# The convolution layer taken in two halves, its MLP under another kind of norm, and a new order of issue at the end of the Fourier layer

## The chip, the cores and the metric

One Trainium2 chip, all 8 cores (two dies of four). Each core computes two of the sixteen sequences and never talks to another core. The metric is the device time of the slowest core, in microseconds (us). A program on all cores falls now and then into a slower state, in which the cores of one die are granted a lower TensorE clock; each run is therefore sorted into fast or slow, and only fast runs are compared. Engines are called as in the profile: PE (matmuls), PEld (its weight loads), DVE (vector engine), ACT (scalar engine), POOL (GpSimd), SP (the engine that issues most transfers here).

## The reference

Four residual layers with the mixers pool, conv, Fourier, pool; behind each mixer there is an MLP with a squared ReLU; each of the two parts has an RMS norm in front. `x` is (16, 2048, 1024). The parts that matter here:

```python
def rms_norm(x, g):
    y = x * lax.rsqrt(jnp.mean(x * x, axis=-1, keepdims=True) + NORM_EPS)
    return y * g

def conv_module(h, w_in, dw, dw_bias, ln_g, ln_b, w_out):
    val, gate = jnp.split(h @ w_in, 2, axis=-1)          # 1024 -> 2 x 1024
    v = val * jax.nn.sigmoid(gate)                       # GLU
    v = depthwise_conv(v, dw) + dw_bias                  # 31 taps, centred, over positions
    mu = jnp.mean(v, axis=-1, keepdims=True)             # LayerNorm over ALL channels
    var = jnp.mean(jnp.square(v - mu), axis=-1, keepdims=True)
    vn = (v - mu) * lax.rsqrt(var + LN_EPS) * ln_g + ln_b
    return jax.nn.silu(vn) @ w_out

def fourier_mixer(h, w_in, w_out):
    u = (h @ w_in).reshape(b, s, 4, 256)
    return jnp.fft.fft2(u, axes=(1, 3), norm='ortho').real.reshape(b, s, d) @ w_out

def sq_relu_mlp(h, w_up, w_down):
    a = jax.nn.relu(h @ w_up)                            # 1024 -> 4096
    return (a * a) @ w_down
# ... (pool mixer, parameters and the loop over the layers cut)
```

The kernel uses bf16 operands with f32 accumulation.

## The kernel before

A sequence lies in SBUF as X, 8 channel chunks of 128 partitions by 2048 positions in f32; work goes by position tiles of 512 (`j` = 0 to 3). A helper records every operation, works out the semaphores, and emits them in the order of the Python calls, one queue for each engine. So the order of calls below is the order on each engine.

The MLP goes through the hidden width in four slabs; a step is one slab of one tile. `up` makes relu squared, `down` adds into X. The norm comes in two kinds. Kind "norm": the tile's statistics must be known first, then eight DVE instructions write scaled copies of X (x times gain times 1/rms) that the matmuls read. Kind "mlp": the matmuls read copies that carry only the gain (`x_chunk`, made as soon as X is written), and since relu squared of a scaled input is relu squared times the square of the scale, the norm is put on afterwards, as a factor `r2` on every down product.

```python
class Mlp:
    def up(self, i, count=FCS):
        # ... (fetch the slab's weights; kind "norm" waits for the statistics here)
        for fc in range(lo, hi):
            bank = b.bank()
            for kc in range(DC):
                b.mm(bank, wu[kc // 4][...], b.Hk(n, j, kc), kc == 0, kc == DC - 1)
            t = b.T.next()
            b.act(t, bank, AF.Relu)
            b.tt(a[:, fc, :], t, t, ALU.mult)
    def down(self, i):
        # ...
        for dc in range(DC):
            # ... (eight matmuls into bank)
            t = bank
            if n.kind == "mlp":
                t = b.TM.next()
                b.tt(t, bank, r2, ALU.mult)
            b.tt(b.X[:, dc, sl], b.X[:, dc, sl], t, ALU.add)
    def run(self):
        b.pump(2); self.up(0)
        for i, (k, j) in enumerate(self.steps):
            if n.kind == "mlp" and k == 0 and j not in n.ready:
                b.x_ready(n, j)               # squares of X on ACT, sums on DVE
            if i + 1 < len(self.steps):
                self.up(i + 1)
            self.down(i)
            # ... (prefetch of weights)
```

The conv layer runs chunk by chunk over all four tiles. The convolution needs each value on shifted partitions, so a chunk's GLU output goes to scratch in DRAM (`scr_v`) and comes back. LayerNorm needs every channel of a tile, hence the tail: sums, normalize (subtract, multiply, Silu) and the output projection come when all convolutions are done.

```python
def conv_layer(self, s, li):
    # ... (glu: 16 matmuls, sigmoid on ACT, product on DVE; spread: write to and read back from scratch)
    for c in range(1, DC - 2):
        # ... build_diag(c - 1); glu(c, j) for all four tiles
        for h in range(2):
            for j in range(h * HT, (h + 1) * HT):
                conv(c - 1, j, v4[h])
            spread(c, h, v4[h])
    # ... (the last two chunks)
    ln_sums(0); ln_rstd(0)
    conv(ca, 2, v4[1]); ln_sums(1); normalize(0, 1)
    # ...
    out(0, lambda: [f() for f in late])       # projection, six banks open at a time
    out(1)
    self.x_ready(self.nxt, 0)
    out(2)
    out(3)
    for j in range(1, NT):
        self.x_ready(self.nxt, j)
```

The end of the Fourier layer interleaves its last projections with the first up products of its MLP:

```python
    for oc in range(DC):
        out_step(1, oc)                       # 9 matmuls, then four adds on DVE
        for j in (1, 2, 3):
            self.x_chunk(nx, j, oc, eng="act")
        self.M.up(0, 1)                       # 8 matmuls, relu on ACT, square on DVE
```

Of the kernel before, what the change touches and what calls it, by code (L numbers as in the profile page):

```python
# [103 lines left out]
def const_tables():  # L104
# [4 lines left out]
    M[:, lay["mask"]:lay["mask"] + 32] = np.tile(np.eye(32), (4, 1))  # L109
# [208 lines left out]
class Mlp:  # L318
    def __init__(self, bld, s, li, n, nxt, order, ahead):
        self.b, self.s, self.li, self.n, self.nxt, self.order, self.ahead = bld, s, li, n, nxt, order, ahead  # L320
        self.steps = [(k, j) for k in range(NSLAB) for j in order]
        self.ups, self.downs, self.fc = {}, {}, {}
        self.A = None

    def up(self, i, count=FCS):
# [13 lines left out]
        for fc in range(lo, hi):  # L339
# [5 lines left out]
            b.tt(a[:, fc, :], t, t, ALU.mult)  # L345
        if hi == FCS and lo < FCS:
            if j == self.order[-1]:
                b.release(self.ups[k])
# [3 lines left out]
    def down(self, i):  # L352
# [23 lines left out]
        if j == self.order[-1]:  # L376
            b.release(self.downs[k])

    def run(self):
# [3 lines left out]
        for i, (k, j) in enumerate(self.steps):  # L383
            if n.kind == "mlp" and k == 0 and j not in n.ready:
                b.x_ready(n, j)
            if i + 1 < len(self.steps):
                self.up(i + 1)
# [10 lines left out]
class Builder:  # L398
# [88 lines left out]
    def make_plan(self):  # L487
# [8 lines left out]
        for s in range(self.nseq):  # L496
            for li, kind in enumerate(KINDS):
# [20 lines left out]
                elif kind == "conv":  # L518
                    win, wo = W[f"l{li}_conv_w_in"], W[f"l{li}_conv_w_out"]
                    for c in range(0, DC, 2):  # L520
                        add(("cin", s, li, c), 1, [
                            ("pool", 0, v * DC * 512, BF16, (DC, 256),
                             rows(win[:, v * D + c * 128:v * D + (c + 2) * 128]), None) for v in range(2)])
                    add(("cwo", s, li), 2, [("pool", h, 0, BF16, (4, D), rows(wo[h * 512:(h + 1) * 512, :]), None)
                                            for h in range(2)])
# [42 lines left out]
    def pump(self, reserve, ahead=6):  # L568
        while (self.w_i < len(self.plan) and len(self.w_got) < ahead and self.plan[self.w_i][0][0] not in ("cwo", "ftab")
               and len(self.freeb) - self.plan[self.w_i][1] >= reserve):  # L570
            self.w_issue()
# [123 lines left out]
    def out_tile(self, j, w, src, eng="dve", lazy=False, hook=None):  # L695
        sl = slice(j * TT, (j + 1) * TT)
        n = self.nxt
        for oc in range(DC):
# [7 lines left out]
        if not lazy:  # L706
# [137 lines left out]
    def conv_layer(self, s, li):  # L844
# [3 lines left out]
        L = HT * TT + 8  # L848
        miscb = self.alloc()
# [8 lines left out]
        acc1b = self.alloc()  # L858
        ACC1 = self.buf(acc1b, F32, (NT, TT))
# [4 lines left out]
        mask = self.cm("mask", 32)  # L864

        def Cv(c, j):
            return self.buf(Cb[c // 2, j // 2], F32, (2, 2, TT))[:, j % 2, c % 2, :]

        def SLv(c, j):
            return self.buf(Cb[c // 2, j // 2], BF16, (2, 2, 2 * TT))[:, j % 2, c % 2, 0:TT]  # L870

        def V4(b, q):
            return self.buf(b, BF16, (4, L))[:, q, :]

        def build_diag(c):
            dwc = self.VEC[:, dwo + c * 32: dwo + (c + 1) * 32]
            self.tt(DGs[c % 2], mask.unsqueeze(1).broadcast_to([128, 32, 32]),
                    dwc.unsqueeze(2).broadcast_to([128, 32, 32]), ALU.mult)

        def win(c):  # L880
            if c // 2 not in slab:
                slab[c // 2] = self.w_get(("cin", s, li, c // 2 * 2))[0]
            return self.buf(slab[c // 2], BF16, (2, DC, 256))[:, :, :, (c % 2) * 128:(c % 2) * 128 + 128]

        def glu(c, j):
            self.need_stat(n, j)
            w = win(c)
# [6 lines left out]
            self.act(sg, bg, AF.Sigmoid)  # L894
            self.tt(Vc[c % 2][:, CONV_PAD + j * TT:CONV_PAD + (j + 1) * TT], bv, sg, ALU.mult)

        def vwrite(c, h):
            w = slice(h * (HT + 1) * TT, VW if h else (HT + 1) * TT)
            self.dma("sp", f"vs{h}", (s, c), self.scr["v"][c % 2][:, w], Vc[c % 2][:, w], writes=[f"v{c % 2}{h}"])

        def vread(c, h, b):
            sc = self.scr["v"][c % 2]
            v4 = self.buf(b, BF16, (4, L))
            for sh in (0, 2, 1, 3):
                src = bass.AP(sc.tensor, sc.offset + h * HT * TT + 8 * sh, [[VW, 32], [32 * VW, 4], [1, L]])
                self.dma("sp", f"v{c % 2}{h}", (s, c), v4[32 * sh:32 * sh + 32], src,
                         reads=[f"v{c % 2}{h}", f"v{c % 2}0"])

        def spread(c, h, b):
            vwrite(c, h)  # L910
            vread(c, h, b)

        def conv(c, j, b, late=None):
            h = j // HT
            if (c // 2, h) not in Cb:
# [556 lines left out]
```

## Time and profile before

| before | value | from |
|---|---|---|
| time, median of 3 runs | 4976.78 us (4974.51 to 5418.52) | the timed runs |
| span of an undisturbed core | about 4964 us, middle one | cores without a dip of the clock, all calls |
| PE busy | 96% | busy line of the page |
| all waits of PE, core 5 | 182 us | its waits |
| clock granted, core 5 | 0.985 | the cores view |
| one full matmul (512 columns) in a dense stretch | 215.8 ns | 400 of them start within 86.3 us |

PE sets the end. "Clock" is the mean clock that TensorE was granted, as a share of full speed. In every view a line such as L407 is that of a helper: 407 is any matmul, 421 any ACT instruction, 424 a two-input DVE or POOL instruction, 428 a one-input one, 432 (438 in the kernel after) a scaled product with three inputs, 442 (448) a memset. In the kernel after, the numbers of the first four are 413, 427, 430 and 434. "arena" is SBUF, "ps" is PSUM.

### The profile page before, as it was taken

Reading aid. Unit: us, or ns where it says so; the run is one execution under the profiler, and the core shown is the slowest. Engines: PE = TensorE matmul, PEld = TensorE weight load, DVE = VectorE, ACT = ScalarE, POOL = GpSimd, SP = SyncE. Lnnn points to the kernel's source line nnn. Section 1 sums busy time; section 2 is a strip of 40 time slices with the busy share of each in tenths; the row PEclk is TensorE's granted clock in tenths of the full one; section 3 lists DMA queues with packets and bytes.
Section 4 is the critical chain, followed back from the end, with each engine's and each line's share of the span. In section 5 each row is a group of like instructions: output and inputs, shape, how many; then the busy total and the mean of one; then the engine's idle time right before and its main releaser. Section 6 shows DMA issues by size and latency. Waiting matters only on the chain.

```text
span 5030.9 us, 67432 instructions; the slowest of 8 cores (4954.5 to 5030.9 us)
## 1 busy us (share of the span) xinstructions
PE 4828.7 (96%) x24270; PEld 2190.0 (44%) x24270; DVE 2647.5 (53%) x3948; ACT 1456.5 (29%) x2139; POOL 197.0 (4%) x218
## 2 busy tenths in 40 slices
PE   7999999899998999999999999979998899999998
PEld 3444444344443444444444444434443344444443
DVE  2433454756655667443455435466657465645345
ACT  4311234611234113411253113353112321233112
POOL 0000000100010000000000000010000000000000
PEclk7888999999999999999999999989999999999999
DMA  7312125411034220512142230444201421123201
GB/s 155 62 34 34 18 56 132 76 34 34 9 112 76 43 42 9 101 34 34 40 145 51 42 43 1 120 84 76 38 22 53 67 43 34 26 34 56 46 1 67
DMA packets 147460, 274.61 MB, mean 55 GB/s; under 512 B 6848, under 2 KB 33600, under 8 KB 145088
## 3 DMA queue, kind: packets, MB, share of 16 engines
q0 software_dynamic: 98752, 164.11, 19.6%
q1 hardware_dynamic: 48384, 106.19, 7.2%
q8 instruction: 202, 3.31, 0.3%
q14 instruction: 122, 1.00, 0.1%
HBM read 398.59 MB, written 33.69 MB: 86 GB/s over the span
## 4 chain that ended last, share of the span: by engine, by line
PE 88%; DVE 5%; DMA 3%; ACT 2%; issue 2%; SPq 0%; POOL 0%; DVEq 0%; ACTq 0%; POOLq 0%
PE ps L407 88%; DVE arena L424 4%; ACT arena L421 2%; DVE arena L432 1%; DMA arena<-l_pool_w_in 1%; DMA arena<-xT 0%; DMA arena<-l_pool_w_out 0%; DMA arena<-scr_v 0%; DMA scr_v<-arena 0%; DMA arena<-l_mlp_up 0%; SPq L445 0%; POOL arena L445 0%; DVE arena L428 0%; ACT L421 0%; DVEq L285 0%
## 5 line engine op out<-in xcount | busy, mean ns | idle before, releaser
L407 PE MATMUL ps<-arena 128*128 128x512 bf16 (+5 forms) x24270 | 4828.7, 377 | 185.4 <-ACT arena L421 67.4
L407 PEld LDWEIGHTS ps<-arena 128*128 128x128 bf16 (+1 forms) x24270 | 2190.0, 99 | 2823.6 <-issue 520.5
L424 DVE TENSOR_TENSOR arena<-arena 128x512 f32<-128x512 f32 (+5 forms) x2044 | 1426.2, 707 | 1285.7 <-ACT arena L421 1208.7
L421 ACT ACTIVATE arena<-ps 128x512 f32<-128x512 f32 (+2 forms) x1368 | 788.0, 596 | 2618.3 <-PE ps L407 2505.7
L424 DVE TENSOR_TENSOR arena<-arena,ps 128x512 f32<-128x512 f32 (+2 forms) x834 | 555.5, 683 | 717.3 <-PE ps L407 697.4
L421 ACT ACTIVATE arena<-arena 128x512 bf16<-128x512 f32 (+3 forms) x490 | 493.0, 1037 | 697.3 <-DVE arena L424 676.5
L424 DVE TENSOR_TENSOR arena<-ps,arena 128x512 f32<-128x512 f32 (+1 forms) x584 | 402.4, 690 | 226.0 <-PE ps L407 202.9
L432 DVE SCALAR_TENSOR_TENSOR arena<-arena 128x512 bf16<-128x512 f32 (+1 forms) x320 | 215.5, 745 | 62.9 <-ACT arena L421 61.2
L421 ACT ACTIVATE arena<-ps,arena 128x512 bf16<-128x512 f32 (+2 forms) x264 | 167.4, 663 | 221.1 <-PE ps L407 204.2
L445 POOL DMA_DIRECT2D arena<-l_mlp_up x64 | 47.8, 750 | 1479.6 <-PE ps L407 1199.6
L445 POOL DMA_DIRECT2D arena<-l_mlp_down x64 | 48.0, 753 | 1405.3 <-PE ps L407 1020.0
L428 DVE TENSOR_SCALAR arena<-arena 128x512 bf16<-128x512 f32 (+1 forms) x144 | 62.7, 470 | 60.9 <-DMA arena<-xT 40.4
L424 POOL TENSOR_TENSOR arena<-arena 128x512 f32<-128x512 f32 (+1 forms) x36 | 61.9, 1722 | 219.1 <-ACT arena L421 158.4
L421 ACT ACT_TABLE_LOAD x17 | 21.8, 1283 | 26.9 <-DMA arena<-xT 14.2
L445 POOL DMA_DIRECT2D arena<-l_conv_w_out x4 | 3.0, 748 | 555.5 <-PE ps L407 555.5
L445 POOL DMA_DIRECT2D arena<-l_conv_w_in x16 | 14.0, 894 | 215.7 <-PE ps L407 215.7
L445 POOL DMA_DIRECT2D arena<-l_pool_w_in x14 | 11.1, 804 | 175.5 <-PE ps L407 174.4
L439 DVE COPY arena<-arena 128x512 f32<-128x512 f32 (+1 forms) x12 | 4.1, 345 | 25.1 <-ACT arena L421 25.1
L442 POOL MEMSET arena<- 128x1024 bf16 (+1 forms) x6 | 4.0, 702 | 280.5 <-DVE arena L424 280.5
L445 POOL DMA_DIRECT2D arena<-l_pool_w_out x4 | 3.0, 759 | 38.9 <-PE ps L407 38.9
L445 POOL DMA_DIRECT2D arena<-l_fourier_w_inT x2 | 1.5, 744 | 67.9 <-PE ps L407 67.9
L445 POOL DMA_DIRECT2D arena<-l_fourier_w_out_x x2 | 1.1, 542 | 72.7 <-DVE arena L424 72.7
(6 smaller groups left out, 2.8 us busy)
## 6 DMA issues: line engine op xcount, KB each, us to landing
arena<-l_mlp_up POOLq DMA_DIRECT2D x64, 1024.0 KB, 11.7
arena<-l_mlp_down POOLq DMA_DIRECT2D x64, 1024.0 KB, 11.3
arena<-scr_v SPq DMA_DIRECT2D x128, 258.0 KB, 4.9
arena<-xT SPq DMA_DIRECT2D x32, 512.0 KB, 8.6
outT<-arena SPq DMA_DIRECT2D x16, 1024.0 KB, 4.3
arena<-l_conv_w_in POOLq DMA_DIRECT2D x16, 512.0 KB, 10.9
arena<-dfts SPq DMA_DIRECT2D x8, 1024.0 KB, 6.2
scr_v<-arena SPq DMA_DIRECT2D x16, 384.0 KB, 2.5
```

Of the source, the lines that this page charges most:

```text
L407: self.P.add("pe", lambda e: e.matmul(out, lhsT, rhs, start=start, stop=stop, skip_group_check=skip), reads=[lhsT, rhs], writes=[out])
L421: self.P.add("act", lambda e: e.activation(out, in_, func, **kw), reads=reads, writes=[out])
L424: self.P.add(eng, lambda e: e.tensor_tensor(out, in0, in1, op), reads=[in0, in1], writes=[out])
L428: self.P.add(eng, lambda e: e.tensor_scalar(out, in0, s1, None, op0), reads=reads, writes=[out])
L432: self.P.add(eng, lambda e: e.scalar_tensor_tensor(out, in0, scalar, in1, op0, op1), reads=reads, writes=[out])
L439: self.P.add(eng, lambda e: e.tensor_copy(out, in_), reads=[in_], writes=[out])
L442: self.P.add(eng, lambda e: e.memset(ap, val), writes=[ap])
L445: return self.P.add(q, lambda e: e.dma_start(out=out, in_=in_), reads=[in_] + list(reads), writes=[out] + list(writes), chan=chan, group=g ...
```

## The change

Its intent has three parts.

1. **Conv layer in two halves.** Tiles 0 and 1 are convolved for all chunks first; then the GLU of tile 3 and the convolutions of tiles 2 and 3 run beside LayerNorm, normalize and projection of the first half, so that PE has matmuls while DVE and ACT work. Sigmoid becomes a tanh (sigmoid(g) = (1 + tanh(g/2))/2, with the half put into the convolution's mask). The diagonals and more of the subtracts go to POOL. The output weights come in two slabs of columns.
2. **The MLP after the conv layer takes kind "norm"**: eight scaled copies per tile before its matmuls, no product on the down banks. Its first up products move into the end of the conv layer to fill holes there. The tile order (0, 3, 1, 2) is left to the last slab.
3. **End of the Fourier layer**: weights asked for earlier, relu before the copies on ACT, the square after the next projection's adds on DVE; in `run`, half of the next up products before the squares of `x_ready`.

```diff
@@ the tables
-    M[:, lay["mask"]:lay["mask"] + 32] = np.tile(np.eye(32), (4, 1))
+    M[:, lay["mask"]:lay["mask"] + 32] = np.tile(0.5 * np.eye(32), (4, 1))
@@ Mlp.up
-            b.tt(a[:, fc, :], t, t, ALU.mult)
+            sq = lambda o=a[:, fc, :], t=t: b.tt(o, t, t, ALU.mult)
+            if later is None:
+                sq()
+            else:
+                later.append(sq)
@@ Mlp.run
-            if n.kind == "mlp" and k == 0 and j not in n.ready:
-                b.x_ready(n, j)
             if i + 1 < len(self.steps):
+                self.up(i + 1, FCS // 2)
+                if n.kind == "mlp" and k == 0 and j not in n.ready:
+                    b.x_ready(n, j)
                 self.up(i + 1)
@@ conv_layer: glu
-            self.act(sg, bg, AF.Sigmoid)
-            self.tt(Vc[c % 2][...], bv, sg, ALU.mult)
+            self.act(sg, bg, AF.Tanh, scale=0.5)
+            self.stt(Vc[c % 2][...], sg, 1.0, bv, ALU.add, ALU.mult)
@@ conv_layer: the second half (what it replaces is cut)
+        ln(0)
+        stepB(0)                      # two convolutions of the second half, diagonal, read back
+        normalize(0, 0, 2)
+        gluB(2)                       # GLU of tile 3, write to scratch
+        stepB(1)
+        normalize(0, 2, 4)
+        # ... (on in this pattern)
+        gluB(1)
+        normalize(0, 6, 8)
+        stepB(4)
+        cwo += self.w_get(("cwo", s, li, 1))
+        out(0, 0, 4, lambda oc: normalize(1, oc, oc + 1))
+        stepB(5)
+        out(0, 4, 8, lambda oc: normalize(1, oc, oc + 1))
+        # ... (prefetch)
+        stepB(6)
+        out(1, 0, 4)
+        self.need_stat(self.nxt, 0)   # statistics and the eight scaled copies of tile 0
+        stepB(7)
+        self.M.up(0, 2)               # first up products of the MLP
+        ln(1)
+        out(1, 4, 8, lambda oc: normalize(2, 2 * oc - 8, 2 * oc - 6))
+        self.M.up(0)
+        out(2, 0, 4, lambda oc: normalize(3, oc, oc + 1))
+        self.need_stat(self.nxt, 1)
+        out(2, 4, 8, lambda oc: normalize(3, oc, oc + 1))
+        self.M.up(1)
+        out(3, 0, 4)
+        self.need_stat(self.nxt, 2)
+        out(3, 4, 8)
@@ four_layer
+        self.pump(2, 1)
         for st in dft_steps(0):
...
+        later = []
         for oc in range(DC):
             out_step(1, oc)
+            if later:
+                later.pop(0)()
+            self.M.up(0, 1, later)
             for j in (1, 2, 3):
                 self.x_chunk(nx, j, oc, eng="act")
-            self.M.up(0, 1)
+        later.pop(0)()
@@ build
-                    row.append(Norm(f"l{li}_norm_mlp", "norm" if kind == "pool" else "mlp", s))
+                    row.append(Norm(f"l{li}_norm_mlp", "mlp" if kind == "four" else "norm", s))
```

Cut: the allocation of buffers, the slabs of the weights, the loops of the first half.

## The prediction

> **What bounds the kernel now.** I read the cores view first, then the page's busy lines, then, on one undisturbed core, the waits of the tensor engine, its busy time by stage, and the timelines where it sits idle.
>
> ```profile
> core 3: 5030.9 us, clock 0.967
> ...
> core 5: 4954.5 us, clock 0.985
> ...
> die 0 (median of its cores): 5022.4 us, clock 0.970
> die 1 (median of its cores): 4966.0 us, clock 0.982
> ```
>
> The profile fell in the slow state: die 0 ran at a lower clock. The fast runs (4976.78 and 4974.51 us) look like die 1, so all stage readings below are of core 5. The page (core 3) says who sets the end:
>
> ```profile
> PE 4828.7 (96%) x24270; PEld 2190.0 (44%) x24270; DVE 2647.5 (53%) x3948; ACT 1456.5 (29%) x2139; POOL 197.0 (4%) x218
> ```
>
> PE is the bound, and the change leaves every matmul in place: the same GLU, convolution, projection and MLP products, in another order. So what can be gained is only time in which PE stands still, and time in which it runs at a reduced clock. The waits of PE on core 5 (engine, line, waited for: total us, times, longest) say how much standing there is:
>
> ```profile
> PE ps L407 <- ACT arena L421: 66.8, 37, 7.0
> PE ps L407 <- DVE arena L424: 56.7, 28, 11.8
> PE ps L407 <- DMA arena<-l_pool_w_in: 16.2, 2, 15.5
> PE ps L407 <- DVE arena L442: 12.6, 2, 10.2
> PE ps L407 <- DMA arena<-scr_v: 12.6, 5, 4.2
> ...
> PE ps L407 <- DMA arena<-l_mlp_up: 5.8, 2, 3.6
> ```
>
> All rows together are 182 us. The clock adds 4954.5 x (1 - 0.985) = 74 us. Everything else, some 4700 us, is matmul streaming and fixed. By stage, core 5 (from:to, length, PE busy, PEld, DVE, ACT, POOL, then the PE clock):
>
> ```profile
> 627.00:779.00 152.00, 145.93 (x1244) 66.92 (x1248) 65.32 (x92) 53.12 (x82) 1.50 (x2) 0.99 0.59 136
> 779.00:905.00 126.00, 99.61 (x598) 41.56 (x591) 87.60 (x117) 88.98 (x117) 28.06 (x25) 0.91 0.36 66
> 1328.00:1362.00 34.00, 24.32 (x268) 16.95 (x266) 30.93 (x63) 17.44 (x34) 0.54 (x1) 0.80 0.42 137
> 1410.00:1500.00 90.00, 75.86 (x412) 34.35 (x410) 51.81 (x80) 39.59 (x62) 5.20 (x7) 0.94 0.51 82
> 3071.00:3228.00 157.00, 149.86 (x1293) 69.15 (x1296) 66.14 (x98) 54.30 (x84) 1.50 (x2) 0.98 0.58 135
> 3228.00:3355.00 127.00, 97.09 (x561) 40.34 (x554) 87.88 (x118) 89.01 (x118) 28.51 (x25) 0.91 0.35 64
> 3775.00:3815.00 40.00, 18.05 (x105) 7.98 (x103) 33.90 (x71) 10.12 (x13) 0.54 (x1) 0.74 0.31 97
> 3865.00:3945.00 80.00, 67.12 (x370) 30.38 (x369) 46.41 (x71) 36.16 (x56) 5.20 (x7) 0.94 0.57 93
> ```
>
> Each core does two sequences, so each stage stands twice. Idle is length minus busy; lost to the clock is length x (1 - clock).
> - Conv layer (rows 1, 2, 5, 6): idle 6.1 + 26.4 + 7.1 + 29.9 = 69.5, clock 1.5 + 11.3 + 3.1 + 11.4 = 27: 97 us. Nearly all is in its end (LayerNorm, normalize, output projection), where DVE and ACT are each some 70% busy and wait on each other in chains.
> - Start of the Fourier layer (rows 3, 7): idle 9.7 + 22.0, clock 6.8 + 10.4: 49 us.
> - End of the Fourier layer (rows 4, 8): idle 14.1 + 12.9, clock 5.4 + 4.8: 37 us.
>
> That is 183 of the 256 us; the rest (first loads, last norm, pool layers) the change does not touch.
>
> [...]in the rows with idle the mean clock is 0.74 to 0.94, in dense stages 1.00[...]. [...]the page of before has 17 loads of mean 1283. [...]Here a 128x512 f32 tensor_tensor takes 1373 ns on POOL and 723 on DVE.
>
> **The change, part by part.**
>
> *1. Conv layer in halves.* Now all four position tiles of all eight channel chunks are convolved before LayerNorm begins, and the projection then has no other matmul beside it. The new order does chunks 0 to 7 for the first half (tiles 0 to 2 of the GLU feed it), then interleaves the second half's GLU and convolutions with LayerNorm, normalize and projection of the first. The durations here come from the groups by shape: 20972 full matmuls in 4648.4 us at a clock of 0.967 make 0.214 us each. Per interleaved pair PE has 16 of them = 3.4, plus two convolution tiles. Those: 2048 small matmuls busy 122.4 us, so 32 take 1.9, two take 3.8. Sum 7.2 us. DVE in that time: GLU product 0.69, four running sums 4 x 0.72, one subtract and two multiplies 2.2: 5.8. ACT: tanh 0.6, four convolution reads 2.6, two Silu 1.5: 4.7. Both fit. The scratch trip (write, read back, median landings 2.5 and 4.9 us; some 12 us from the last GLU matmul to the first convolution) has 3.4 + 10.2 = 13.6 us of GLU before its first use and 10.7 or more later. So the five waits on it should go or fall under 1 us. Tanh instead of sigmoid avoids a table switch at each alternation; the half goes into the mask at no cost. POOL takes the diagonal builds and more subtracts.
>
> *2. The MLP after conv changes its norm.* Before, it scaled each down product by the norm on DVE: 8 instructions for each of 16 steps, two sequences, 256 x 0.69 = 177 us of DVE, beside matmuls that take 1.7 us each group. Now eight scaled copies per tile (8 x 0.67 = 5.4 us DVE) come before its first matmul (eight of them took 5.38 in the timeline). The MLP itself gains nothing in its middle, as PE is already full there. But at its end DVE is behind: on core 5 PE finishes at 3778.7 and DVE drains the last bank only at 3785.7. With 0.69 instead of 1.38 us per bank this 7 us backlog shrinks to 1, so the Fourier layer's inputs are ready some 6 us earlier.
>
> *3. End of the Fourier layer.* There the loop period is 5.5 us (x_chunk copies before the relu on ACT, its square before the next adds on DVE), while PE needs 17 x 0.213 = 3.6; PE runs out of banks. The new order (relu before copies, square after the next adds) leaves DVE 5 x 0.70 = 3.5 us and ACT 2.7. The earlier issue of the weights takes away the 3.6 and 2.2 us on l_mlp_up.
>
> *What remains in the conv layer, per sequence (estimates).*
> - Second half of the output weights: issued by POOL only after the diagonal that follows a convolution; about 2.5 + 9.6 to landing against 10.6 us of matmuls: 2 idle, 1 clock.
> - First MLP tile: after 10.6 us of PE work the stat matmul, then table load 1.3, Ln and Exp 1.3, DVE already 1 us late, eight copies 5.4, against 3.8 of convolution and a first group of 1.7: 3.6 idle, 1.7 clock.
> - Second LayerNorm behind the same DVE queue: 1.
> - Second MLP tile: the same chain behind Silu and a table load, against 6.8 us of matmuls: 4.7 idle, 2 clock.
> - First convolution: 1.
>
> Together 17 us, 34 for two.
>
> *Sum.* Conv 97 - 34 = 63. Fourier end 37 - 4 = 33. Fourier start: 5.5 idle and 3.5 clock of the second sequence, some 7 and 4 of the first, where the backlog also holds the banks of the setup matmuls: 20. Total 116 us, and 4977 - 116 = 4861.
>
> **The rivals.**
> - *The end of the conv layer becomes DVE-bound.* From the first projection on, DVE has 32 adds (22), 24 multiplies and 4 subtracts (20), 12 sums (9), 24 copies (16), four square reductions of 2.55 (10) and 16 relu squares (11): 88 us, against PE's 54.6 + 11.5 + 27.3 = 93. At 95% in-order coupling can cost far more than I charge. If each of three tiles waits its full chain of some 10 us, cold clock included, little of the conv gain is left: about 4920. For: the table. Against: two weight groups of the MLP are moved there to fill just this hole.
> - *Tanh is not in Silu's set.* Then five alternations bring ten loads, 13 us of ACT per layer, and ACT's 4.7 per pair grows to 7.3 against 7.2: up to 10 us per layer, 4880.
> - *The scratch trip or the weights stay exposed*, as one order on one queue now carries all of them: 3 to 4 us per hit plus clock, 4875.
> - *The filling is perfect*: nothing of the 34 left, and the Fourier start gains more: 4815.
>
> **Range and chances.** The 2% line is 4877, only 16 us from my centre, and the conv remainder of 34 is the softest term; it would have to be 50 to lose the line. The Fourier end I trust within 5 us, the start within 8. Range 4825 to 4908; faster by over 2% 0.68, within 2% 0.31, slower 0.01, as nothing new is long enough to cost more than 183 us.
>
> **What would show it.** Right: PE's waits on an undisturbed core fall from 182 to about 105 us, its clock rises from 0.985 to about 0.992, waits on l_mlp_up vanish, those on scr_v fall to a few us, DVE busy falls by some 150 us, the 128x512 bf16 scaled copies of a norm go from 256 to 320 (and 64 GLU products join that group), the Fourier start still shows some 16 us idle in the second sequence. Wrong: table loads far above 30, PE waiting 7 us or more on DVE's scaled copies before the first MLP groups, or on l_conv_w_out, or the Fourier loop still at 5 us a turn. A clock of 0.81 in both dies for long would void the comparison, not the reasoning.

What no trace or run of this case shows is cut from this text: a rule for the clock with a price per us of idle, a filing of functions in tables, and a ratio for POOL. (The 17 loads that it names are table loads of ACT.) The clock terms for what is foreseen are estimates. Where they rest on idle, they agree with the rows of before: 128 us of idle and 55 of clock are 0.43 us of clock for each us of idle, so 0.9, 1.5 and 2.0 for the idle of 2, 3.6 and 4.7 us, where it has 1, 1.7 and 2; at the Fourier start 17.2 for 31.7 are 0.54, so 6.8 for the 12.5 us of idle that it expects to go, where it has 7.5. That tanh avoids table switches was assumed; e4 counts them.

## The result, and the profile after

The kernel after takes 4893.29 us (median of 10 runs, 4890.16 in the fastest), before 4976.89 us in the same rounds. The ratio of the fast runs is 0.9833, 95% interval 0.9821 to 0.9844: 1.7% less time, inside the 2% band, to which the prediction had given 0.31 (and 0.68 to a gain of more than 2%). Ratios here are the mean time of one kernel's fast runs over that of the other's of the same rounds, so not quite the ratio of the medians. The outputs are correct.

So the predicted 4861 was 32 us too low, though inside its range (4825 to 4908), and of the 116 us that were expected 84 came. By spans of undisturbed cores (cores whose mean clock shows no dip), which leave out how the slowest of eight is drawn, it is 4964 to 4887: 77 us.

The profile after is of core 4. The busy line of the page:

```profile
PE 4753.1 (97%) x24270; PEld 2164.4 (44%) x24270; DVE 2506.7 (51%) x3724; ACT 1415.5 (29%) x2077; POOL 283.5 (6%) x262
```

The same 24270 matmuls, DVE busy 141 us less (150 foreseen). The waits of PE on core 4 (engine, line, waited for: total us, times, longest):

```profile
PE ps L413 <- ACT arena L427: 27.7, 25, 3.0
...
PE ps L413 <- DVE arena L430: 17.3, 12, 5.4
...
PE ps L413 <- DVE arena L438: 9.8, 12, 2.9
PE ps L413 <- DMA arena<-l_conv_w_out: 8.6, 2, 4.6
PE ps L413 <- DMA arena<-scr_v: 2.6, 3, 1.0
```

Set beside the rows of before: the two large ones, on ACT and on DVE's two-input work, fell from 66.8 and 56.7 to 27.7 and 17.3; the scratch row fell from 12.6 to 2.6; the row of the MLP's up weights is gone. Two rows are new: the scaled copies (L438, 9.8) and the output weights of the conv layer (8.6). All rows, with those left out (first loads, pool layers, one-input work of DVE, a memset at the Fourier start), sum to 116 us, where 105 were foreseen. But 11 us of waits don't make up 32 or 39 us, so the waits alone don't tell the story. Busy time of core 4 by stage (from:to, length, PE, PEld, DVE, ACT, POOL, PE clock, DMA share, GB/s), rows in the order of those of before:

```profile
631.00:785.00 154.00, 151.81 (x1287) 68.25 (x1289) 76.13 (x106) 64.51 (x100) 26.78 (x15) 1.00 0.54 125
785.00:912.00 127.00, 113.33 (x648) 47.67 (x641) 98.25 (x132) 67.08 (x85) 38.72 (x27) 0.92 0.35 67
1322.00:1356.00 34.00, 27.20 (x297) 16.98 (x295) 25.00 (x57) 17.34 (x38) 0.00 (x0) 0.90 0.63 214
1404.00:1494.00 90.00, 88.87 (x478) 40.85 (x477) 60.64 (x92) 42.13 (x65) 4.45 (x6) 0.98 0.43 71
2991.00:3195.00 204.00, 202.33 (x1527) 90.94 (x1529) 108.53 (x150) 83.50 (x119) 31.02 (x17) 1.00 0.41 94
3195.00:3322.00 127.00, 112.40 (x641) 46.82 (x634) 98.08 (x132) 67.52 (x85) 39.02 (x27) 0.93 0.36 67
3732.00:3772.00 40.00, 24.34 (x132) 10.79 (x131) 24.98 (x57) 11.19 (x17) 1.48 (x2) 0.79 0.54 169
3818.00:3898.00 80.00, 78.87 (x432) 36.31 (x431) 55.34 (x85) 37.71 (x60) 4.45 (x6) 0.98 0.50 80
```

Rows 4 and 8, the end of the Fourier layer, are nearly closed: 1.1 us of idle each, where 14.1 and 12.9 stood. Rows 1 and 5, the body of the conv layer, are dense. Rows 2 and 6, its end, are not: 13.7 and 14.6 us of idle, and the clock is still 0.92 and 0.93, hardly above the 0.91 of before. Row 7, the second Fourier start, keeps 15.7 us of idle.

Idle plus clock, as the prediction summed them, is a rough measure of loss, as will be seen. A better one comes from the start times of the matmuls in the trace: the time from the first to the last start of a stage, less what its matmuls take in a dense stretch, by their pace in the traces from start to start: 215.8 ns for 512 columns, 55 to 62 for 128 to 143, 25.6 for up to eight, and a quarter of 215.8 for the packed ones of the convolution (in after, core 4, forty of them start in the 2.16 us from 3233.14 us, four at a time). It's worked out from the traces, not an answer of the profile; every later verdict by stage uses it. The numbers are the middle of the undisturbed cores of the profiled run (they mostly lie within 3 us of it; before's Fourier end is the exception, with 34.5, 39 and 43 on its three). The conv layer is counted with the start of its MLP.

| lost us, both sequences | conv layer | Fourier start | Fourier end | sum |
|---|---|---|---|---|
| before (the prediction had 97, 49, 37: 183) | 99 | 39 | 39 | 177 |
| foreseen for after | 34 | 29 | 4 | 67 |
| after | 63 | 27.5 | 8.5 | 99 |
| gain foreseen | 63 | 20 | 33 | 116 |
| gain measured | 36 | 11.5 | 30.5 | 78 |

The gains sum to 78 us, about what the spans say (77). So the shortfall lies in the conv layer (27 us) and at the Fourier start (8.5 us); the Fourier end came out as foreseen.

At that end the timeline shows the new loop. Before, core 5 (start, duration, engine, line, operation; in brackets what ended the idle time before it):

```profile
1452.55 0.69 DVE L424 TENSOR_TENSOR arena<-arena 128x512 bf16<-128x512 f32 x1 [2.01 <-ACT arena L421]
...
1458.10 0.69 DVE L424 TENSOR_TENSOR arena<-arena 128x512 bf16<-128x512 f32 x1 [2.01 <-ACT arena L421]
```

After, core 4:

```profile
1436.86 0.60 ACT L427 ACTIVATE arena<-ps 128x512 f32<-128x512 f32 x1 [1.35 <-PE ps L413]
...
1440.53 0.60 ACT L427 ACTIVATE arena<-ps 128x512 f32<-128x512 f32 x1 [1.24 <-PE ps L413]
```

The square of one turn to that of the next took 5.55 us before, and DVE stood 2.01 us for ACT in each turn. After, relu follows relu in 3.67 us, which is 17 matmuls of 215.8 ns, and the relu waits for PE: PE sets the pace.

At the end of the conv layer the timeline of core 4, sequence 2, shows where PE stands:

```profile
3236.52 5.38 DVE L438 SCALAR_TENSOR_TENSOR arena<-arena 128x512 bf16<-128x512 f32 x8
3237.51 0.38 PE L413 MATMUL ps<-arena 128*128 128x512 bf16 x1 [1.60 <-DVE arena L438]
3238.07 0.38 PE L413 MATMUL ps<-arena 128*128 128x512 bf16 x1 [0.18 <-DVE arena L438]
...
3273.31 0.38 PE L413 MATMUL ps<-arena 128*128 128x512 bf16 x1 [2.74 <-ACT arena L427]
...
3285.54 6.69 PE L413 MATMUL ps<-arena 128*128 128x512 bf16 x12 [2.88 <-DVE arena L438]
```

Eight copies take 5.38 us, 0.67 each, and the first group of the MLP takes its matmuls one by one behind them: the second starts 0.56 us after the first, the next ones 0.66 us apart, where 0.216 would do in a dense stretch. The record of each says 0.38 busy, so of 0.34 to 0.44 us lost per matmul only 0.18 to 0.29 are in the waits; the rest passes as busy. The last line has twelve matmuls in 6.69 us, shown as busy without a gap: by their start times eight stand 0.66 us apart behind the copies, and the last of the twelve follow at 0.43, twice the dense 0.216. This is why the row of L438 reads a modest 9.8 us.

### The profile page after: what moved, and what is told of

It is laid out like the page before. It is cut to its first block, busy times and chain, and to the rows that moved or that the text cites. A ratio compares the mean times of both kernels' runs of the same rounds, so it can differ in the third digit from the quotient of the medians.

```text
span 4888.7 us, 67048 instructions; the slowest of 8 cores (4878.4 to 4888.7 us)
## 1 busy us (share of the span) xinstructions
PE 4753.1 (97%) x24270; PEld 2164.4 (44%) x24270; DVE 2506.7 (51%) x3724; ACT 1415.5 (29%) x2077; POOL 283.5 (6%) x262
## 4 chain that ended last, share of the span: by engine, by line
PE 90%; DVE 3%; DMA 3%; ACT 2%; issue 2%; POOL 0%; SPq 0%; DVEq 0%; ACTq 0%; POOLq 0%
PE ps L413 90%; DVE arena L430 2%; ACT arena L427 2%; DVE arena L438 1%; DMA arena<-l_conv_w_out 1%; DMA arena<-xT 1%; DMA arena<-l_pool_w_in 1%; DMA arena<-l_pool_w_out 0%; DMA arena<-scr_v 0%; ACT L427 0%; DMA scr_v<-arena 0%; POOL arena L451 0%; SPq L451 0%; DMA outT<-arena 0%; DVEq L285 0%
## 5 line engine op out<-in xcount | busy, mean ns | idle before, releaser
L413 PE MATMUL ps<-arena 128*128 128x512 bf16 (+5 forms) x24270 | 4753.1, 371 | 119.2 <-ACT arena L427 27.7
L413 PEld LDWEIGHTS ps<-arena 128*128 128x128 bf16 (+1 forms) x24270 | 2164.4, 98 | 2707.4 <-issue 223.7
L430 DVE TENSOR_TENSOR arena<-arena 128x512 bf16<-128x512 f32 (+5 forms) x1756 | 1245.2, 720 | 1193.3 <-ACT arena L427 1145.9
L430 DVE TENSOR_TENSOR arena<-arena,ps 128x512 f32<-128x512 f32 (+1 forms) x1090 | 729.5, 684 | 874.5 <-PE ps L413 854.7
L427 ACT ACTIVATE arena<-arena 128x2048 bf16<-128x2048 f32 (+3 forms) x424 | 453.0, 1090 | 641.2 <-DVE arena L430 620.0
L438 DVE SCALAR_TENSOR_TENSOR arena<-arena 128x512 bf16<-128x512 f32 (+1 forms) x384 | 258.5, 745 | 77.3 <-ACT arena L427 75.5
L430 DVE TENSOR_TENSOR arena<-ps,arena 128x512 f32<-128x512 f32 x264 | 181.9, 689 | 46.9 <-PE ps L413 39.3
L430 POOL TENSOR_TENSOR arena<-arena 128x512 f32<-128x512 f32 (+2 forms) x80 | 147.9, 1871 | 680.6 <-PE ps L413 582.9
L438 DVE SCALAR_TENSOR_TENSOR arena<-arena,ps 128x512 bf16<-128x512 f32 x64 | 44.0, 690 | 104.2 <-PE ps L413 88.6
L427 ACT ACT_TABLE_LOAD x21 | 26.9, 1283 | 42.2 <-DVE arena L430 16.2
L445 DVE COPY arena<-arena 128x512 f32<-128x512 f32 (+1 forms) x12 | 6.9, 576 | 15.7 <-ACT arena L427 15.7
## 6 DMA issues: line engine op xcount, KB each, us to landing
arena<-l_mlp_down POOLq DMA_DIRECT2D x64, 1024.0 KB, 11.5
```

The costliest lines, as they stand in the source:

```text
L413: self.P.add("pe", lambda e: e.matmul(out, lhsT, rhs, start=start, stop=stop, skip_group_check=skip), reads=[lhsT, rhs], writes=[out])
L427: self.P.add("act", lambda e: e.activation(out, in_, func, **kw), reads=reads, writes=[out])
L430: self.P.add(eng, lambda e: e.tensor_tensor(out, in0, in1, op), reads=[in0, in1], writes=[out])
L438: self.P.add(eng, lambda e: e.scalar_tensor_tensor(out, in0, scalar, in1, op0, op1), reads=reads, writes=[out])
L445: self.P.add(eng, lambda e: e.tensor_copy(out, in_), reads=[in_], writes=[out])
```

## The experiments

Twelve kernels were run. All outputs were correct. Beside the ratio I give the middle span of those cores whose clock shows no dip (before: 4964, after: 4887), since in several runs a pair of cores dipped; see e8. The four calls ran on four chips; before's middle span was 4964 or 4965 on each, so spans of different calls are compared. A difference of spans under 3 us I don't read.

### e1_fourier_end: part 3 alone, on the kernel before

```diff
 run:        -  x_ready ahead of up(i + 1)
             +  up(i + 1, FCS // 2), x_ready, up(i + 1)
 four_layer: +  self.pump(2, 1) before the transforms
             +  relu before the copies; square after the next adds   (as in the diff above)
```

> Only the end of the Fourier layer is changed in the kernel before (weights issued earlier, relu ahead of the scaled copies, the square after the next adds, the MLP's first step split). The prediction's accounting, which adds each stretch's idle time and its whole clock deficit, says 33 us less, about 4944. My accounting from the start times of successive matmuls, in which a low clock costs nothing while the engine stands, says 27 us less, about 4950. Both want the waits on l_mlp_up gone.

Measured: ratio 0.9945 [0.9907, 0.9982], span 4933, 31 us under before. Lost at the Fourier end 8 us instead of 39; conv layer and Fourier start as before (98 and 39.5). No row on the MLP's up weights is left among PE's waits. The step "33 us at the Fourier end" stands.

### e2_norm_kind: part 2's norm alone, on the kernel before

```diff
-  row.append(Norm(f"l{li}_norm_mlp", "norm" if kind == "pool" else "mlp", s))
+  row.append(Norm(f"l{li}_norm_mlp", "mlp" if kind == "four" else "norm", s))
   and the tile order (0, 3, 1, 2) only in the last slab
   and prefetch reserves raised to 6 and 9 buffers
```

The reserves had to be raised, by the author's account because the program as first built ran out of buffers. That makes weights come later, so this is not quite the norm alone.

> Only the norm of the MLP after the conv layer is changed in the kernel before (eight scaled copies per tile before the MLP in place of 256 products on VectorE, and the tile order that goes with it). The DVE backlog at the start of the Fourier layer should shrink: 20 us gained by the prediction's accounting, 11 by mine. Against it stands the seam between the conv layer and its MLP, where in this order of work nothing hides the copies of the first tile: a loss of 5 to 10 us. Net: prediction's accounting 10 to 15 us less, mine within 6 us of the kernel before.

Measured: ratio 1.0043 [1.0012, 1.0074], span 4988, 24 us *over* before. The Fourier start lost 27.5 us instead of 39, the gain of 11.5 that the whole change shows there. But the conv layer with the start of its MLP lost 137 instead of 99. The row of the scaled copies among PE's waits on core 5 (the line numbers of this kernel are one higher than in before):

```profile
PE ps L408 <- DVE arena L433: 21.1, 16, 3.9
```

In before the products of this line make PE wait nowhere. Beside it the waits on the MLP's up weights rose from 5.8 to 11.3 us, which may come from the raised reserves, so some 6 of the 38 us may be laid to them. The rest says: in the old order the copies (with the tile order that goes with them) stand in front of the MLP and cost far more than they bring.

### e3_no_fourier_end: the change without part 3

```diff
 (the edit of e1_fourier_end taken back, on the kernel after)
```

> The changed kernel without its new end of the Fourier layer. If the parts add up, this is 84 minus 27 = 57 us less than before (about 4920) by my accounting, and 84 minus 33 = 51 us less (4926) by the prediction's. A large departure from both would mean that the parts lean on each other.

Measured: ratio 0.9887 [0.9864, 0.9911], span 4914, 50 us under before. With the 31 of e1 that makes 81, where the whole change gives 77: the parts add up within 4 us. So what is missing from the prediction isn't an interplay with the Fourier end; it lies within parts 1 and 2.

### e4_sigmoid: the change with sigmoid instead of tanh

```diff
-            self.act(sg, bg, AF.Tanh, scale=0.5)
-            self.stt(Vc[c % 2][...], sg, 1.0, bv, ALU.add, ALU.mult)
+            self.act(sg, bg, AF.Sigmoid)
+            self.tt(Vc[c % 2][...], bv, sg, ALU.mult)
   and the mask without its factor 0.5
```

> The changed kernel with sigmoid in place of tanh. If the exchange was made to keep one table for gate and Silu, there are some 10 more table loads per conv layer (21 become about 40), 13 us more of ScalarE per layer, which has 4.7 us of work in 7.2 us there: 5 to 20 us slower than the changed kernel (4898 to 4913). If the table is not what matters, the time stays at 4893.

Measured: ratio 0.9878 [0.9848, 0.9908], span 4910, 23 us over after. The table loads in the groups of after, then of this kernel:

```profile
L427 ACT ACT_TABLE_LOAD x21 | 26.9, 1283 | 42.2 <-DVE arena L430 16.2 <-DMA arena<-xT 14.3 <-PE ps L413 11.5
```

```profile
L427 ACT ACT_TABLE_LOAD x33 | 42.3, 1283 | 71.2 <-DVE arena L430 45.8 <-DMA arena<-xT 13.2 <-PE ps L413 11.9
```

Twelve loads more, six per sequence, 15.4 us of ACT, and 23 us of time: here a load costs more than its own 1283 ns (88.5 us lost in the conv layer instead of 63). So beside Silu the tanh spares loads that sigmoid brings, 21 against 33. The rival "Tanh is not in Silu's set" has fallen, and the tanh is worth 23 us of what the change brings.

### e5_wout_early: the second slab of output weights asked for one step sooner

```diff
-        stepB(4)
         cwo += self.w_get(("cwo", s, li, 1))
+        stepB(4)
```

> The changed kernel with the second half of the output weights asked for one step earlier, so that GpSimd issues it ahead of a diagonal build. The trace of the changed kernel shows waits of 1.0 to 4.2 us on l_conv_w_out, twice a run. Theory: that wait is a real part of what the conv layer still loses, so 4 to 8 us less than the changed kernel (4885 to 4889). Rival: the conv tile and products behind it wait for the DVE chains anyhow, and the time stays at 4893.

Measured: ratio 0.9824 [0.9805, 0.9844], span 4881, 6 us under after; lost in the conv layer 60.5 instead of 63. The wait was real (4.6 us at its longest where the prediction allowed 2), and small.

### e6_double_copies: the eight scaled copies of the conv layer's MLP written twice

```diff
                     for c in range(DC):
                         self.stt(self.Hk(n, j, c), self.X[:, c, sl], ..., r, ALU.mult, ALU.mult)
+                    for c in range(DC if n.gname == "l1_norm_mlp" else 0):
+                        self.stt(self.Hk(n, j, c), self.X[:, c, sl], ..., r, ALU.mult, ALU.mult)
```

> The changed kernel with the eight scaled copies per tile before the conv layer's MLP written twice (same values). Theory: the copies of tiles 0 and 1 lie on the path of the tensor engine, those of tiles 2 and 3 do not; so 2 x 5.4 us per sequence, 21 to 26 us in all with the clock, slower than the changed kernel (4914 to 4919). Rival, that DVE as a whole is the bound at the end of the conv layer: all four tiles count, 43 us or more (4936 or above). If nothing of the chain were on the path: 4893.

Measured: span 4910, 23 us over after; ratio 0.9934 [0.9892, 0.9975], where four of the six runs have pairs of cores in a dip, so I go by the span. The row of the scaled copies among the waits of core 1 (9.8 us in after):

```profile
PE ps L413 <- DVE arena L438: 30.3, 4, 8.7
```

So copies are on the path that sets the end: of 43 us of added DVE work (64 copies of 0.67), 23 reach the time, about the copies of the first two tiles of each sequence (4 x 5.4 = 21.5). The four waits of the row stand at 831, 885, 3254 and 3307 us, before the first and the second tile of each sequence, as the theory says.

### e7_four_banks: four up banks open at once, so that each copy feeds four matmuls

```diff
-        for fc in range(lo, hi):
-            bank = b.bank()
+        if wide:
+            banks = {fc: b.bank() for fc in range(lo, hi)}
             for kc in range(DC):
+                for fc in range(lo, hi):
+                    b.mm(banks[fc], wu[...], b.Hk(n, j, kc), kc == 0, kc == DC - 1)
...
-        self.M.up(0, 2)
+        self.M.up(0, 4, wide=True)
...
+        self.M.up(1, 4, wide=True)
         self.M.up(1)
```

> The changed kernel, in which the first four column groups of the first and second MLP tile run through the eight row chunks together in four banks, instead of one group after the other. A chunk then gives four matmuls (0.86 us) for each scaled copy (0.67 us) instead of one, so PE no longer stutters behind the copies. Theory: some 3 to 4.5 us less at each of the two tiles, 12 to 18 us in all less than the changed kernel (4875 to 4881). Rival: only the start of the chain counts, not its pace: within 4 us of 4893.

Measured: span 4877, 10 us under after (12 to 18 were expected); lost in the conv layer 56 instead of 63. Ratio 0.9837 [0.981, 0.9864], again with pairs in a dip; its undisturbed runs took 4882.9 to 4885.0 us. The stutter is thus worth 7 to 10 us for both sequences: part of the missing 27, not all.

### e8_defer_squares: the squares of the MLP's second tile moved behind its first up products

```diff
-        out(1, 4, 8, lambda oc: normalize(2, 2 * oc - 8, 2 * oc - 6))
+        out(1, 4, 8, lambda oc: normalize(2, 2 * oc - 8, 2 * oc - 6), ready=False)
         self.M.up(0)
+        self.x_ready(self.nxt, 1)
```

> The changed kernel with the squares and their reduction of the second tile moved behind the rest of the first MLP tile. In the changed kernel ScalarE is kept 3.8 us by the squares and DVE 2.6 by the reduction, and PE then waits 2.7 us for banks, a term that the prediction left out. Theory: this wait goes, 5 to 8 us less in two sequences (4885 to 4888). Rival: the chain of the second tile starts later for it and the time stays within 3 us of 4893.

Measured: span 4882, 5 us under after, but the loss in the conv layer is 63, as in after. Ratio 0.9882 [0.9839, 0.9925], useless here: of its fast runs only one (4887.25 us) is undisturbed. By the stage account nothing was gained: the 2.7 us wait on ACT, which the prediction had not listed, turned into waits elsewhere. The span's 5 us I can't place; taken together, inconclusive.

This run shows the dips best. Busy time of the same 400 us of dense MLP on cores 2 and 0:

```profile
2000.00:2400.00 400.00, 400.00 (x1728) 175.39 (x1727) 167.70 (x245) 74.90 (x119) 9.94 (x13) 0.93 0.25 42
```

```profile
2000.00:2400.00 400.00, 398.05 (x1818) 181.37 (x1854) 180.79 (x266) 82.59 (x130) 9.51 (x13) 1.00 0.22 40
```

The clock column reads 0.93 against 1.00, the mean clock of the run is 0.977 and 0.976 on cores 2 and 3 and 0.991 on cores 0 and 1, and the records show cores 2 and 3 at 0.81 for 160 us from about 1993 us, and once more from about 2594 us, some 30 us of time each; cores 0 and 1 of the same die have none of it. A run with such a pair can still be sorted as fast, since the dies differ by less than the mark. It happened with several kernels, before among them. Hence the spans of undisturbed cores.

### e9_all: five repairs at once

```diff
   e7_four_banks + e5_wout_early + e8_defer_squares
-        gluB(1)
         normalize(0, 6, 8)
+        gluB(1)
...
-        out(1, 0, 4)
-        self.need_stat(self.nxt, 0)
+        out(1, 0, 4, lambda oc: self.need_stat(self.nxt, 0) if oc == 2 else None)
```

> The changed kernel with four small repairs at the end of the conv layer at once: output weights earlier, four banks for the first MLP groups, the second tile's squares later, the first tile's statistic one product group earlier, and the last two normalizations of the first tile ahead of a GLU tile. The repairs one by one gave 5, 10 and 3 us on undisturbed cores; if the waits are separate pieces of one path, 20 us or more less than the changed kernel, core spans near 4864 against 4886. If they are one wait that moves from place to place, not more than the best of them, 4875.

Measured: ratio 0.9811 [0.9795, 0.9826], median 4881.9, span 4874, 13 us under after, where 20 or more were expected if the losses were separate. (The text above counts four repairs and lists five.) The conv layer still loses 53. The two measures disagree on what this says. By spans the three repairs that were also run alone (6, 10 and 5) sum to 21, and 13 came: waits that move into one another. By stage they sum to 2.5 + 7 + 0 = 9.5, and 10 came: they add, and the two new repairs bring nothing that can be seen. Whether it is one chain is thus not shown.

### e10_old_norm: the new conv layer with the old norm

```diff
-                    row.append(Norm(f"l{li}_norm_mlp", "mlp" if kind == "four" else "norm", s))
+                    row.append(Norm(f"l{li}_norm_mlp", "norm" if kind == "pool" else "mlp", s))
   and e5_wout_early; the end re-ordered, as tiles now need no statistics before up:
+        out(1, 0, 4)
         ln(1)
         out(1, 4, 8, lambda oc: normalize(2, 2 * oc - 8, 2 * oc - 6), ready=False)
         self.M.up(0)
+        self.x_ready(self.nxt, 0)
+        out(2, 0, 8, lambda oc: normalize(3, oc, oc + 1), ready=False)
         self.M.up(1)
+        self.x_ready(self.nxt, 1)
+        out(3, 0, 8, ready=False)
```

> The changed conv layer, but with the norm of its MLP as in the kernel before (the scaled copy needs no statistic; the factor is multiplied in on DVE after each down product), with the order at the end of the conv layer fitted to it. Theory: the statistic and its eight copies at the seam cost more there (some 10 to 13 us per sequence) than the lighter MLP gives back at the start of the Fourier layer (11.7 us for both): the conv layer loses some 15 to 20 per sequence instead of 29, the Fourier start 31 for both instead of 20, net 8 to 15 us less than the changed kernel, core spans 4871 to 4878. Rival: the change of norm is what makes the new order fit; without it other waits take its place and spans are at or above 4886.

Measured: ratio 0.981 [0.9794, 0.9825], median 4880.5, span 4871, 16 us under after and 10 under e5_wout_early. Lost: conv layer with the start of its MLP 41 (e5_wout_early: 60.5), Fourier start 39.5 (e5_wout_early: 27.5). So the new norm, with the order that it asks for, costs some 20 us in the conv layer and brings 12 at the Fourier start, for both sequences: a net loss of 8, by spans 10. The two can't be told apart here: the edit also changes when squares are taken and when the MLP's weights are asked for. The prediction had both sides in its sums, 20 us of gain at the start and 24 us of cost in its two terms for the MLP's tiles (3.6 + 1.7 and 4.7 + 2, twice), and never set one against the other.

Its largest remaining wait that is new was on the first down weights of the MLP (11.5 us in two waits on core 5).

### e12_old_norm_tuned: e10 with two waits taken out

```diff
-        gluB(1)
         normalize(0, 6, 8)
+        gluB(1)
...
         self.x_ready(self.nxt, 1)
+        self.w_want(("mlpd", s, li, 0))      # first down weights asked for earlier
         out(3, 0, 8, ready=False)
```

> The variant with the old norm in the new conv layer, with two waits taken away that its trace shows: 1.9 us for the last normalizations of the first tile, 2.5 us for the first down weights (issued before the last projection now). Theory: both lie on the path, 4 to 8 us less in two sequences, core spans near 4862 against 4868. Rival: they move to the next wait, 4868.

Measured: span 4858 over 30 undisturbed cores, 29 us under after, 106 under before, 2.1%. Only two of six runs were fast, 4864.07 and 4861.78 us, so no ratio with an interval is given; of before's six fast runs the two without a dip took 4970.75 and 4974.15 us, and the quotient of the means is 4862.9 / 4972.5 = 0.978. Two stages of core 5 of this kernel, the conv layer's ends:

```profile
785.00:912.00 127.00, 122.75 (x725) 56.07 (x714) 93.92 (x125) 81.06 (x117) 40.72 (x30) 1.00 0.55 97
3195.00:3322.00 127.00, 123.60 (x658) 55.50 (x657) 91.27 (x124) 74.34 (x106) 34.80 (x27) 0.99 0.45 75
```

Here the clock is 1.00 and 0.99, and 4.3 and 3.4 us of idle are left. The conv layer loses 24 us instead of 63; the Fourier start is back at 40. It is faster than both kernels.

### e13_pool_adds: e12 with the adds of the last slab on POOL

```diff
+            far = KINDS[self.li] == "conv" and k == NSLAB - 1
-            b.tt(b.X[:, dc, sl], b.X[:, dc, sl], t, ALU.add)
+            b.tt(b.X[:, dc, sl], b.X[:, dc, sl], t, ALU.add, eng="pool" if far else "dve")
```

> The same, with the add into the residual moved from DVE to GpSimd in the last quarter of the MLP after the conv layer, where the old norm gives DVE two instructions per bank. Theory: the Fourier layer's start is late because DVE is behind there, so with one DVE instruction per bank it loses 20 to 23 us for both sequences instead of 31, and the run is 8 to 11 us shorter, core spans near 4852. Rival: GpSimd, at 1.37 us or more per add against 1.7 us of matmuls per bank[...], becomes the late one: no gain or a loss.

Measured: one fast run of seven, 4857.95 us; span 4852 over 22 undisturbed cores, 6 under e12. The stage account finds 3 of them, at the Fourier start (37 instead of 40). Expected were 8 to 11 if the backlog of DVE sets that start; it is mostly the rival, as the trace shows: on core 1, in the second sequence, PE's last MLP matmul ends at 3690.9 us and the last add on POOL at 3696.3. POOL is 5.4 us behind, where DVE was 7.0 behind in before. So the run exchanges one backlog for another and does not test what an empty one would bring.

What else holds the Fourier start can be read in the trace of before (core 5, sequence 2), from the end of DVE's backlog at 3785.7 to the first matmul of the next dense stretch:

```profile
3785.78 1.91 ACT L421 ACTIVATE arena<-arena 128x2048 bf16<-128x2048 f32 x1 [4.03 <-DVE arena L424]
3787.79 2.55 DVE L424 TENSOR_TENSOR arena<-arena 128x2048 bf16<-128x2048 bf16 x3 [2.10 <-ACT arena L421]
3790.26 5.38 DVE L432 SCALAR_TENSOR_TENSOR arena<-arena 128x512 bf16<-128x512 f32 x8
3795.56 5.45 DVE L424 TENSOR_TENSOR arena<-arena 128x511 bf16<-128x511 bf16 x16
3801.25 14.10 PE L407 MATMUL ps<-arena 128*128 128x512 bf16 x86 [10.18 <-DVE arena L442]
```

The last squares, their reduction, eight copies and sixteen sums (and a memset, L442) take 15.6 us one after the other, and a smaller backlog leaves them as they are: in after, with the lighter MLP, 15.7 us of idle are left there (row 7 above).

## Why the prediction was right or wrong, point by point

**Right: what bounds the kernel, the Fourier end, and the scratch trip.** PE sets the end, and all of the gain is standing and slow time of PE, in the three places named. The Fourier end gave 30 to 31 us of the 33, alone (e1) and in the whole (e3), with the loop at 17 matmuls a turn. Tanh spares table loads (21, and 33 with sigmoid; e4). The waits on scratch fell to 2.6 us, the waits on the MLP's up weights are gone, DVE's busy time fell by 141 us. Less well: PE's waits fell to 116 us (105 foreseen) and the clock rose to 0.989, the mean of both dies in fast runs (0.992 foreseen). Of its own signs of being wrong, waits of 7 us or more on the scaled copies or on l_conv_w_out, two came true if a whole run is meant (9.8 and 8.6 us), and none if a single wait is (2.9 and 4.6).

**Wrong: the term "Together 17 us, 34 for two" of "What remains in the conv layer".** It measured 31 to 32 us per sequence, 63 for both. The prediction called it the softest term. Its parts, on core 4 in sequence 2, as waits of PE alone:

| what remains, one sequence | idle foreseen | wait seen |
|---|---|---|
| second half of the output weights | 2 | 4.6 |
| first MLP tile | 3.6 | 3.1 |
| second LayerNorm | 1 | about 0 |
| second MLP tile, squares and statistics | not listed | 2.7 |
| second MLP tile, copies | 4.7 | 3.4 |
| first convolution | 1 | 1.0 |
| sum | 12.3 | about 15 |

The waits were nearly right in kind and in size. What was missed is the rest: against 4.7 us for the clock, some 15 us per sequence passed as busy time. The start times of the matmuls in the trace divide it (core 4; first and second sequence):

| lost us in the conv layer | sequence 1 | sequence 2 |
|---|---|---|
| recorded waits, all | 15.9 | 16.3 |
| matmuls 0.66 us apart behind the copies, beyond their recorded waits | 4.3 | 4.6 |
| matmuls 0.43 us apart without a wait, twice the dense 0.216 | 5.9 | 5.1 |
| end of the matmul before a wait, booked as busy (some 0.2 each) | 1.8 | 1.5 |
| small losses in the convolutions and the rest | 3.4 | 3.3 |
| sum | 31.2 | 30.8 |

So what the prediction had wrong is mostly what goes on between the waits. The 0.43 us pace is its clock term, at 5 to 6 us where it had 4.7: the clock records of the trace stand at 0.5 in just these stretches, 3.4 or 6.8 us at a time. What it had no term for is the stutter behind the copies, with its waits some 7 us per sequence; e7 takes it away (at most 0.8 us of it are left), waits elsewhere grow by some 2 to 3 us, and 7 to 10 us are gained for both sequences. In e12 both are nearly gone: at most 0.8 us of stutter and 1.7 at half pace per sequence.

**Wrong: the whole loss of clock was added to the idle.** At the Fourier start the prediction added idle (31.7) and clock (17.2) to 49 us. The account by matmul starts gives 39: 15 in the first sequence, where 16.5 were charged, and 24 in the second, where 32.4 were. Three stretches of the second Fourier start in before, core 5, show why (same columns as above):

```profile
3778.70:3790.00 11.30, 0.02 (x1) 0.00 (x0) 8.11 (x13) 5.03 (x4) 0.54 (x1) 0.73 0.61 195
3790.00:3801.20 11.20, 0.59 (x1) 0.10 (x1) 11.13 (x27) 1.32 (x2) 0.00 (x0) 0.50 0.08 15
3801.20:3815.00 13.80, 13.75 (x86) 6.40 (x87) 11.16 (x28) 3.77 (x7) 0.00 (x0) 0.89 0.32 109
```

The low clock falls almost wholly in the first two, in which PE runs two matmuls. Only the third has work at a reduced clock: 13.8 x (1 - 0.89) = 1.5 us, where 10.4 were charged for the whole. Here a slow clock (0.73 and 0.50 for 22.5 us) while PE stood cost nothing; the mean clock of a stage must be read with where in it the work lies. In the first sequence the waits are short (3.2 us at most) with matmuls between them, and the sum was nearly right. In the conv layer it was right too (97 against 99), but partly by luck: beyond the idle, core 5 lost 10 us by matmuls at half pace and not 27; the ends of matmuls before its 36 waits (7 us) and small losses in the convolutions (12 us) made up the rest.

The gain at the Fourier start, 11.5 instead of 20, was therefore mis-sized twice. The clock, charged at 7.5, gave some 2. The idle fell by 9.2 us (31.7 to 22.5) and not by 12.5: 6.3 in the second sequence, where the shrinking backlog was said to give 5.5, but only 2.9 in the first, where 7 were foreseen. What was foreseen to be left, 29, is about what is left, 27.5.

**The rivals.** "Tanh is not in Silu's set" is rejected (21 loads, where sigmoid has 33; e4). "The scratch trip or the weights stay exposed" holds for the weights, at 3 to 6 us for both sequences (e5). "The end of the conv layer becomes DVE-bound" is rejected for DVE as a whole (of 43 us of added DVE work 23 reached the time, e6) and holds in a milder form: the copies of the first two tiles are on the path. "The filling is perfect" is rejected for the change, but e12 comes near to it at the end of the conv layer, by another way: 4.3 and 3.4 us of idle in its two stages. Its time, 4862 to 4864 us, is still far from the rival's 4815.

**What the prediction didn't ask:** whether part 2 pays at all. With its order it costs some 20 us where it puts the copies ahead of PE and brings 12 where it shortens DVE's backlog (e10 against e5); in the old order it's a loss of 24 (e2, with some of that from the raised reserves). Parts 1 and 3 with the old norm and a few small repairs (e12) save 106 us. The old norm keeps DVE busy for 134 us more (2640.5 us in e12, 2506.7 in after); these lie beside dense matmuls, and the only cost that the stage account shows for them is the 12 us at the Fourier start.

**Open:** where e8's 5 us of span come from; whether the repairs of e9 add up; how much of e10's gain is the norm and how much the order; what an empty backlog would bring at the Fourier start with the old norm; and what makes pairs of cores dip.

## What to carry to other kernels

Price a reduced clock only where matmuls run: split a stage at its waits before adding idle and clock (at the second Fourier start 10.4 us were charged for it and 1.5 counted). Work that an engine off the critical path did beside dense matmuls was nearly free here (134 us more of DVE in e12, 12 us of cost), so trading it for less work that stands between two matmuls can be a loss; ask of each moved instruction who waits for it. Where matmuls came one by one behind another engine's instructions, the trace booked much of the loss as busy (0.66 us apart, 0.38 of it booked, where 0.216 is the dense pace), so count matmuls per time and not only the waits.
